# A hybrid attention layer on one core: its first projection block in another order, and the conditioning weights in smaller pieces

## The chip, the cores and the metric

The kernel runs on one core of one Trainium2 chip. Its time is the device time of one execution in microseconds; where several executions are given, the median counts. The profile is a hardware trace of one execution.

## The reference

One decoder layer on a sequence of 1,024 tokens with 1,024 channels, in float32. Cut to what matters here:

```python
mod = silu(c) @ w_ada + b_ada                      # 1024 x 6144: six vectors of 1024
shift_m, scale_m, gate_m, shift_f, scale_f, gate_f = split(mod, 6)
h    = rms(x) * (1 + scale_m) + shift_m            # adaLN: a row norm, then a scale and shift per channel
proj = h @ w_in                                    # 1024 x 4104: fq fk fv og (512 each), 8 forget logits, rq rk rv rg (512 each)
fox  = forgetting_attention(rms(fq) * g, rms(fk) * g, fv, log_sigmoid(logits + b))   # 8 heads of 64
fox  = rms(fox) * gain * sigmoid(og)
ret  = retention(rope(rq), rope(rk), rv)           # 4 heads of 128, chunks of 128
ret  = rms(ret) * gain * silu(rg)
x    = x + gate_m * (concat(fox, ret) @ w_out)
h    = rms(x) * (1 + scale_f) + shift_f
x    = x + gate_f * (square(relu(h @ w_mlp_in)) @ w_mlp_out)
```

## The kernel before, in words

Tokens are worked on in eight tiles of 128 (t = 0 to 7). Channels are split in eight slices of 128 (k = 0 to 7). A large product is done in three passes, to keep float32 accuracy: each operand is split into a rounded part and a rest (`split_w` for weights: ScalarE casts, VectorE or GpSimd subtracts, lines 133 to 135), and TensorE multiplies high by high, high by low and low by high (lines 295 to 297). A projection group (`proj_group`, line 279) takes four token tiles and 512 columns: for each k it splits one weight slice of 128x512 and runs 4 x 3 matmuls into four PSUM banks. The weights arrive two slices at a time, by SyncE's queue, into two buffers (`raw`); the split slices have five buffers (`f4`).

The input to the projections is `hT[k]`, the normalised and modulated input, turned so that channels lie on the partitions, in a rounded part and a rest. Tile t of x gets its row norm (`norm_x`: squares on ScalarE, the factor by a power on GpSimd, the product on VectorE). `make_hT(k, half)` then turns four tiles of slice k by TensorE, scales and shifts them on ScalarE with the two adaLN columns of k (`mod(0, k)`, `mod(1, k)`), casts on VectorE and subtracts on GpSimd.

The first block is the group rg. Its first half (tiles 0 to 3) needs the adaLN columns of shift_m and scale_m, slice by slice: `first_stage(k)` loads further weights, multiplies the eight rows of `ada_m[k]` (1 MB) by silu(c) and adds them up on VectorE (`ada_sum`, lines 207 to 211, and line 562), sums over the partitions by one-column matmuls (line 217), adds the bias (line 219) and calls `make_hT(k, 0)`. `ahead` runs this one slice ahead of the matmuls. The second half (tiles 4 to 7) only needs `make_hT(k, 1)`. Each half ends with `evac_rg` for its tiles: a sigmoid on ScalarE, a product on VectorE, a product with the gain on GpSimd (lines 384 to 386).

The other four adaLN vectors (16 MB of weights) are not needed until much later. `ada_stages` (line 221) makes eight pieces of 512 columns, each in two loads of 1 MB by SyncE's queue into two buffers (`mr`), with their sums on VectorE (lines 233 to 235), one-column matmuls (line 243) and a bias (line 245). Hooks at each k of the groups rq, rk and rv call these steps one after the other (`todo`, line 523).

The order of instructions on each queue is set by a planner that lists them by program order and by when it expects them to be ready; so steps of the adaLN pieces come earlier than the program writes them. Only the attention part is written as a fixed order (`manual_schedule`, line 860). After the first block come the forget logits (line 410), the groups rq, rk and rv (with rope on GpSimd and VectorE, lines 370 to 373), then the other groups, attention, the output projection and the MLP.

Of the kernel before, what the change touches and what calls it, by code (L numbers as in the profile page):

```python
# [11 lines left out]
F32 = mybir.dt.float32  # L12
# [37 lines left out]
def tile_block(  # L50
# [89 lines left out]
    pT = ctx.enter_context(tc.tile_pool(name="pT", bufs=2, space=PSUM))  # L140
# [9 lines left out]

    def tbank(name):
        return pT.tile([P, CH], F32, tag="T", name=name)
# [23 lines left out]
    early, xg = [], [None] * 4  # L176
# [8 lines left out]
    def load_first_w():  # L185
        wr = raw([P, 2, CH], "wr_first")
        Q.dma_start(wr, win_v[:, 0:2, OFF_R + 3 * RW : OFF_R + 4 * RW])
        early.append(wr)

    load_ada_m(0)  # L190
    load_x(0)
    load_x(1)
    load_first_w()
    load_ada_m(1)
    load_ada_m(2)
    load_ada_m(3)
# [8 lines left out]
    def ada_sum(w):  # L205

        for j in range(2):
            V.tensor_scalar(w[:, j], w[:, j], c_act[:, j : j + 1], None, op0=ALU.mult)
        for j in range(2, 8):
            a = w[:, j % 2]  # L210
            V.scalar_tensor_tensor(a, w[:, j], c_act[:, j : j + 1], a, op0=ALU.mult, op1=ALU.add)

    def ada_cols(w, ms, k, n):
        ps = xbank(f"mps{ms[0]}_{k}")
        for i, m in enumerate(ms):
            for j in range(n):
                T.matmul(ps[:, i : i + 1], w[:, j, i, :], ones, start=(j == 0), stop=(j == n - 1))
        for i, m in enumerate(ms):
            V.tensor_tensor(mod(m, k), ps[:, i : i + 1], bT[:, 8 * m + k : 8 * m + k + 1], op=ALU.add)

    def ada_stages(m, kq):


        ws = []

        def load(a):
            w = mr([P, 4, CH], f"wa{m}_{kq}{a}")
            Q.dma_start(w, wada_v[:, 4 * a : 4 * a + 4, m * D + kq * CH : m * D + (kq + 1) * CH])
            ws.append(w)

        def sums(a):
            w = ws[a]
            V.tensor_scalar(w[:, 0], w[:, 0], c_act[:, 4 * a : 4 * a + 1], None, op0=ALU.mult)
            for j in range(1, 4):
                V.scalar_tensor_tensor(
                    w[:, 0], w[:, j], c_act[:, 4 * a + j : 4 * a + j + 1], w[:, 0], op0=ALU.mult, op1=ALU.add
                )

        def cols_():
            ps = xbank(f"mps{m}_{kq}")  # L240
            for i in range(4):
                for a in range(2):
                    T.matmul(ps[:, i : i + 1], ws[a][:, 0, i * P : (i + 1) * P], ones, start=(a == 0), stop=(a == 1))
            at = slice(8 * m + 4 * kq, 8 * m + 4 * kq + 4)
            V.tensor_tensor(mcol[:, at], ps[:, 0:4], bT[:, at], op=ALU.add)

        return load, sums, cols_

    def norm_x(t):
        xt = xg[t // 2][:, t % 2, :]  # L250
        rr = r_x[:, t : t + 1]
        A.activation(ra([P, D], f"xsq{t}"), xt, AF.Square, accum_out=rr)
        V.tensor_scalar(rr, rr, 1.0 / D, EPS, op0=ALU.mult, op1=ALU.add)
        rsqrt_(rr, 1)
        V.tensor_scalar(xt, xt, rr, None, op0=ALU.mult)

    hT = {}

    def make_hT(k, half):

        if k not in hT:
            hT[k] = s8([P, 2, S], f"hT{k}", F32R)
        ht = hT[k]
        tp = rbank(f"tp{k}_{half}")
        for i in range(4):
            t = 4 * half + i
            T.transpose(tp[:, i * P : (i + 1) * P], xg[t // 2][:, t % 2, k * P : (k + 1) * P], ident)
        h32 = t2([P, CH], f"h32_{k}_{half}")
        A.activation(h32, tp, AF.Identity, bias=mod(0, k), scale=mod(1, k))
        hs = slice(half * CH, (half + 1) * CH)  # L270
        V.tensor_copy(ht[:, 0, hs], h32)
        G.tensor_tensor(ht[:, 1, hs], h32, f32(ht[:, 0, hs]), op=ALU.subtract)
# [6 lines left out]
    def proj_group(name, col, half, evac, hook=None, banks=None):  # L279
# [3 lines left out]
        for k in range(NK):  # L283
            if hook:
                hook(k)
            if k % 2 == 0:
                wr = early.pop(0) if early else load_win(k, col, f"{name}{half}")
            ws = f4([P, 2, CH], f"ws_{name}{half}_{k}", F32R)
            split_w(wr[:, k % 2, :], ws[:, 0, :], ws[:, 1, :], G if name == "rg" and half == 0 else V)
# [233 lines left out]
    todo = [[] for _ in range(5 * 8 + 4)]  # L523
    for n in range(8):
        load, sums, cols_ = ada_stages(2 + n // 2, n % 2)
        todo[5 * n] += [lambda load=load: load(0)]
        todo[5 * n + 2] += [lambda load=load: load(1), lambda sums=sums: sums(0)]
        todo[5 * n + 4] += [lambda sums=sums: sums(1)]
        todo[5 * n + 6 if n < 7 else -1] += [cols_]
# [15 lines left out]
    def ahead(stage):  # L545
        def go(k):
            if k == 0:
                stage(0)
            if k + 1 < NK:
                stage(k + 1)  # L550

        return go

    def first_stage(k):
        if k == 2:
            load_x(2)
        if k == 3:
            load_x(3)
        if k + 4 < NK:
            load_ada_m(k + 4)  # L560
# [5 lines left out]
    for t in range(4):  # L566
        norm_x(t)
# [551 lines left out]
```

## Time and profile before

| | us |
|---|---|
| median of three runs | 1442.01 (1440.3 to 1445.68) |
| the profiled execution | 1444.74 |
| its span in the trace | 1442.9 |

| engine | busy us | share of the span |
|---|---|---|
| TensorE (PE) | 1376.8 | 95% |
| TensorE weight loads (PEld) | 1122.7 | 78% |
| VectorE (DVE) | 636.2 | 44% |
| ScalarE (ACT) | 425.1 | 29% |
| GpSimd (POOL) | 463.9 | 32% |

Busy times are unions of the instructions' intervals; PE's matmuls overlap each other, so the start of one to the start of the next tells the pace. The clock that is granted to TensorE has two levels; a mean between them says how much of a stretch was at which. SP is SyncE, whose queue issues the DMAs. A time in brackets at the end of a line is the idle time of the engine just before it, with what ended it.

### The profile page before, as it was taken

The numbers are of one execution on the slowest core, as the hardware profiler recorded it, in microseconds if no ns is written. First come the engines' busy times: TensorE is split into PE (matmuls) and PEld (weight loads), VectorE is DVE, ScalarE is ACT, GpSimd is POOL, SyncE is SP. The second block draws the span as 40 slices with busy tenths as digits, with TensorE's granted clock in tenths as the row PEclk, the third lists the DMA queues.
The fourth block names the chain that finished last, engine by engine and source line by source line (L and its number), as shares of the span: only waits on it lengthen the run. The fifth ranks groups of instructions, "written<-read, shape, count | busy, mean of one in ns | idle before, by whom it ended". The sixth has DMA issues, their size and how long they took to land.

```text
span 1442.9 us, 17046 instructions
## 1 busy us (share of the span) xinstructions
PE 1376.8 (95%) x6581; PEld 1122.7 (78%) x6581; DVE 636.2 (44%) x1123; ACT 425.1 (29%) x757; POOL 463.9 (32%) x428
## 2 busy tenths in 40 slices
PE   4699898999999889999999999999999999999998
PEld 3477777888888667678778888888888888888887
DVE  6974777445443457753682222322223222122221
ACT  2332212233333357652343311133112321123210
POOL 3456733136452012322562421124301242013420
PEclk9889998999999989999999999999999999999999
DMA  9747446543346644942231111111112111111121
GB/s 286 218 125 168 137 115 186 126 98 117 85 128 148 166 117 118 285 176 74 89 102 30 59 46 56 44 45 59 44 44 58 45 44 57 47 44 51 52 103 59
DMA packets 109953, 146.09 MB, mean 101 GB/s; under 512 B 7624, under 2 KB 61976, under 8 KB 108848
## 3 DMA queue, kind: packets, MB, share of 16 engines
q1 hardware_dynamic: 109872, 145.00, 35.3%
q8 instruction: 52, 0.85, 0.2%
q14 instruction: 29, 0.24, 0.0%
HBM read 122.85 MB, written 10.60 MB: 92 GB/s over the span
## 4 chain that ended last, share of the span: by engine, by line
PE 54%; DVE 2%; POOL 1%; issue 0%; ACT 0%; DMA 0%; DVEq 0%; POOLq 0%; ACTq 0%
PE up L1035 8%; PE up L1036 8%; PE up L1037 8%; PE po_dn L936 8%; PE po_dn L934 8%; PE po_dn L935 8%; PE po_woA L935 1%; PE po_woA L934 1%; PE po_woA L936 1%; DVE xr L980 1%; PE av L734 1%; POOL x L944 0%; PE pt L725 0%; DVE x L940 0%; PE h2p L987 0%
## 5 line engine op out<-in xcount | busy, mean ns | idle before, releaser
L936 PE MATMUL po_dn<-ws_dn,u 128*128 128x512 f32 x512 | 199.3, 389 | 0.0
L935 PE MATMUL po_dn<-ws_dn,u 128*128 128x512 f32 x512 | 199.2, 389 | 0.0
L934 PE MATMUL po_dn<-ws_dn,u 128*128 128x512 f32 x512 | 198.0, 389 | 0.0
L1035 PE MATMUL up<-h,wuh 128*128 128x512 f32 x496 | 193.7, 391 | 0.0
L1036 PE MATMUL up<-h,wuh 128*128 128x512 f32 x496 | 193.4, 390 | 0.0
L1037 PE MATMUL up<-h,wul 128*128 128x512 f32 x496 | 193.2, 390 | 0.0
L1043 POOL TENSOR_TENSOR u<-rl,u 128x512 fp32r<-128x512 f32 x64 | 82.3, 1287 | 325.2 <-ACT u L1042 325.2
L135 DVE TENSOR_TENSOR ws_dn<-wr_dn,ws_dn 128x512 fp32r<-128x512 f32 x64 | 55.2, 862 | 204.8 <-ACT ws_dn L134 204.8
L927 POOL TENSOR_TENSOR wr_dn<-wr_dn,gf 128x512 f32<-128x512 f32 x64 | 85.9, 1364 | 155.1 <-DMA wr_dn<-in_w_mlp_out_dram 155.1
L935 PEld LDWEIGHTS po_dn<-ws_dn,u 128*128 128x128 f32 x512 | 96.1, 188 | 20.0
L936 PEld LDWEIGHTS po_dn<-ws_dn,u 128*128 128x128 f32 x512 | 96.1, 188 | 19.9
L934 PEld LDWEIGHTS po_dn<-ws_dn,u 128*128 128x128 f32 x512 | 96.1, 188 | 19.9
L134 ACT CAST ws_dn<-wr_dn 128x512 fp32r<-128x512 f32 x64 | 39.7, 620 | 242.8 <-PE po_dn L936 216.4
L1036 PEld LDWEIGHTS up<-h,wuh 128*128 128x128 f32 x496 | 93.4, 188 | 19.4
L1035 PEld LDWEIGHTS up<-h,wuh 128*128 128x128 f32 x496 | 93.4, 189 | 19.2
L1037 PEld LDWEIGHTS up<-h,wul 128*128 128x128 f32 x496 | 93.2, 188 | 19.3
L131 POOL TENSOR_TENSOR sm<-sm 128x8 f32<-128x8 f32 (+2 forms) x48 | 59.3, 1241 | 146.8 <-DVE sm L500 56.6
L135 DVE TENSOR_TENSOR wul<-wu,wuh 128x1024 fp32r<-128x1024 f32 x31 | 39.8, 1284 | 139.8 <-ACT wuh L134 111.1
L1041 DVE SCALAR_TENSOR_TENSOR rl<-up,rl 128x512 f32<-128x512 f32 x64 | 43.9, 687 | 110.7 <-ACT rl L1040 110.7
L134 ACT CAST wuh<-wu 128x1024 fp32r<-128x1024 f32 x31 | 32.7, 1054 | 123.2 <-PE up L1036 73.1
L1040 ACT ACTIVATE rl<-up 128x512 f32<-128x512 f32 x64 | 38.0, 594 | 95.6 <-PE up L1037 95.6
L940 DVE TENSOR_TENSOR x<-po_dn,x 128x512 f32<-128x512 f32 x64 | 41.6, 684 | 54.5 <-PE po_dn L936 54.5
(273 smaller groups left out, 2727.0 us busy)
## 6 DMA issues: line engine op xcount, KB each, us to landing
wa<-in_w_ada_dram SPq DMA_DIRECT2D x16, 1024.0 KB, 10.0
wu<-in_w_mlp_in_dram SPq DMA_DIRECT2D x32, 512.0 KB, 4.2
wr_dn<-in_w_mlp_out_dram SPq DMA_DIRECT2D x32, 512.0 KB, 3.5
wam<-in_w_ada_dram SPq DMA_DIRECT2D x16, 512.0 KB
x<-in_x_dram SPq DMA_DIRECT2D x8, 512.0 KB, 7.7
wr_rq<-in_w_in_dram SPq DMA_DIRECT2D x8, 512.0 KB, 6.1
wr_rk<-in_w_in_dram SPq DMA_DIRECT2D x8, 512.0 KB, 4.1
wr_rv<-in_w_in_dram SPq DMA_DIRECT2D x8, 512.0 KB, 5.0
```

The lines of the kernel that those rows point to most:

```text
L131: G.tensor_tensor(ap, ap, mhalf.to_broadcast([P, n]), op=ALU.pow)
L134: A.copy(h_ap, raw_ap)
L135: eng.tensor_tensor(l_ap, raw_ap, f32(h_ap), op=ALU.subtract)
L927: G.tensor_tensor(w, w, gate[:, cs_], op=ALU.mult)
L934: T.matmul(ps[t], lh, ws[:, 0, :], start=(kk == 0), stop=False)
L935: T.matmul(ps[t], lh, ws[:, 1, :], start=False, stop=False)
L936: T.matmul(ps[t], ll, ws[:, 0, :], start=False, stop=(kk == nk - 1))
L1035: T.matmul(ps, wh[:, k, :], hh, start=(k == 0), stop=False)
L1036: T.matmul(ps, wh[:, k, :], hl, start=False, stop=False)
L1037: T.matmul(ps, wl[:, k, :], hh, start=False, stop=(k == NK - 1))
L1041: V.scalar_tensor_tensor(rl, ps, 0.0, rl, op0=ALU.max, op1=ALU.mult)
L1043: G.tensor_tensor(u[:, 1, hs], rl, f32(u[:, 0, hs]), op=ALU.subtract)
```

## The change

The first block takes six token tiles (`FIRST`) through all eight slices and then the other two (`REST`), and is written as a fixed order on all five queues, SyncE's too. The products of the adaLN rows 0 and 1 by silu(c) go from VectorE to ScalarE (`ada_mul`); the two partial sums are added by the one-column matmuls, which are twice as many per slice. Tiles 4 and 5 of a slice are turned, scaled and split after tiles 0 to 3. VectorE does the six accumulations of slice n + 1 two by two between the casts of slice n. GpSimd subtracts for the weights in the first pass, VectorE in the second. The group's weights are loaded twice, as before.

The other adaLN vectors come in 16 pieces of 256 columns, each one load of 1 MB (eight rows), issued by ScalarE, behind what is written before it on that queue; loads, sums and column matmuls are called by the same hooks, at steps 2.5 apart. Some small loads of constants are held behind what is written before them on SyncE's queue. The two banks of the PSUM pool pT are taken strictly in turn (`Ta`, `Tb`).

```diff
+    turn_t = ["Tb", "Ta"]
     def tbank(name):
-        return pT.tile([P, CH], F32, tag="T", name=name)
+        turn_t.append(turn_t.pop(0))
+        return pT.tile([P, CH], F32, tag=turn_t[0], name=name)
...
     def ada_stages(m, kq):
+        w = mr([P, 8, 2 * P], f"wa{m}_{kq}")
+        def load():
+            at = m * D + kq * 2 * P
+            tc.keep_in_program_order(A.dma_start(w, wada_v[:, :, at : at + 2 * P]))
+        def sums():
+            V.tensor_scalar(w[:, 0], w[:, 0], c_act[:, 0:1], None, op0=ALU.mult)
+            for j in range(1, 8):
+                V.scalar_tensor_tensor(w[:, 0], w[:, j], c_act[:, j : j + 1], w[:, 0], op0=ALU.mult, op1=ALU.add)
         def cols_():
             ps = xbank(f"mps{m}_{kq}")
+            for i in range(2):
+                T.matmul(ps[:, i : i + 1], w[:, 0, i * P : (i + 1) * P], ones, start=True, stop=True)
...
+    for n in range(16):
+        todo[5 * n // 2].append(begin)                                        # load
+        todo[5 * n // 2 + 3].append(lambda stages=stages: stages[1]())        # sums
+        todo[5 * n // 2 + 5].insert(0, lambda stages=stages: stages[2]())     # columns
...
+    FIRST, REST = range(6), range(6, 8)
+    def ada_mul(k):
+        w = ada_m[k]
+        for j in range(2):
+            A.mul(w[:, j], w[:, j], c_act[:, j : j + 1])
+    def ada_acc(k, js):
+        w = ada_m[k]
+        for j in js:
+            V.scalar_tensor_tensor(w[:, j % 2], w[:, j], c_act[:, j : j + 1], w[:, j % 2], op0=ALU.mult, op1=ALU.add)
+    def ada_mps(k):
+        mp_of[k] = xbank(f"mps{k}")
+        for m in range(2):
+            for j in range(2):
+                T.matmul(mp_of[k][:, m : m + 1], ada_m[k][:, j, m, :], ones, start=(j == 0), stop=(j == 1))
...
+    with tc.manual_schedule(engines={ENG.PE, ENG.Activation, ENG.DVE, ENG.Pool, ENG.SP}):
...
+        times("rg0", 0, range(4))
+        turn_x(0, (4, 5), xbank)
+        scaled(0, (4, 5))
+        split_h(0, (4, 5))
+        for k in range(NK):
+            n = k + 1
+            if n < NK:
...
+                turn_x(n, range(4), tag_bank("Ta"))
+                ada_mps(n)
+                ada_add(n)
+                scaled(n, range(4))
+                split_first_w("rg0", n, G)
+                if n + 1 < NK:
+                    ada_mul(n + 1)
+                    ada_acc(n + 1, range(2, 4))
+                split_h(n, range(4))
             if k == 0:
+                times("rg0", 0, (4, 5))
+            else:
+                times("rg0", k, (0, 1))
+            if n < NK:
+                turn_x(n, (4, 5), xbank)
+                scaled(n, (4, 5))
+                if n + 1 < NK:
+                    ada_acc(n + 1, range(4, 6))
+                split_h(n, (4, 5))
+                if n + 1 < NK:
+                    ada_acc(n + 1, range(6, 8))
+            if k:
+                times("rg0", k, range(2, 6))
...
+            if k == 7:
+                load_first_w("rg1", 2)
+                for m in range(2):
+                    turn_x(m, REST, (tag_bank("Ta"), xbank)[m])
+                    scaled(m, REST)
+                    split_h(m, REST)
+                    split_first_w("rg1", m, V)
+        tabs["ret"] = load_gain(ret_gain)
+        for t in FIRST:
+            evac_rg(t, ps_of[t])
+        for t in REST:
+            ps_of[t] = bank(f"pp_rg_{t}")
+        for k in range(NK):
+            if k + 2 < NK:
+                if k in (2, 4):
+                    load_first_w("rg1", k + 2)
+                turn_x(k + 2, REST, (tag_bank("Ta"), xbank)[k % 2])
+                scaled(k + 2, REST)
+                split_h(k + 2, REST)
+                split_first_w("rg1", k + 2, V)
+            times("rg1", k, REST)
+        for t in REST:
+            evac_rg(t, ps_of[t])
+    tc.keep_in_program_order(Q.dma_start(rc, rconst))
```

The helpers `square`, `factor`, `norm`, `turn_x`, `scaled`, `split_h`, `split_first_w` and `times` hold the instructions of `norm_x`, `make_hT`, `split_w` and the three matmuls, one step each.

## Rows read from the trace of the kernel before

**Rows 1.** Windows by stage: PE, PEld, DVE, ACT, POOL busy, clock, DMA.

```profile
20.30:79.90 59.60, 43.13 (x178) 33.26 (x177) 53.26 (x109) 18.00 (x29) 25.65 (x21) 0.86 0.84 247
...
84.30:108.70 24.40, 24.36 (x105) 20.14 (x105) 17.94 (x23) 6.32 (x10) 11.72 (x9) 0.93 0.41 84
...
116.70:271.00 154.30, 143.03 (x658) 118.44 (x658) 109.23 (x154) 32.53 (x55) 70.90 (x56) 0.94 0.54 147
```

**Rows 2.** Timeline of DVE and POOL, first block: start, us, engine, line.

```profile
21.40 2.45 DVE L211 SCALAR_TENSOR_TENSOR wam<-wam,sm 128x256 f32<-128x256 f32 x6
...
64.44 4.50 DVE L211 SCALAR_TENSOR_TENSOR wam<-wam,sm 128x256 f32<-128x256 f32 x6
...
64.33 2.74 POOL L135 TENSOR_TENSOR ws_rg<-wr_rg,ws_rg 128x512 fp32r<-128x512 f32 x2
```

**Rows 3.** Windows and timeline where DVE is full and TensorE waits.

```profile
150.00:161.00 11.00, 6.99 (x24) 5.31 (x23) 10.89 (x15) 0.77 (x2) 9.25 (x13) 0.84 0.15 38
...
227.00:238.00 11.00, 11.00 (x40) 9.30 (x40) 10.96 (x12) 0.99 (x2) 10.43 (x8) 0.65 0.78 259
...
219.84 0.48 DVE L233 TENSOR_SCALAR wa<-wa,sm 128x512 f32<-128x512 f32 x1 [7.88 <-DMA wa<-in_w_ada_dram]
...
223.26 0.35 PE L243 MATMUL mps<-sm,wa 128*128 128x1 f32 x2 [2.84 <-issue]
...
226.45 3.15 PE L243 MATMUL mps<-sm,wa 128*128 128x1 f32 x14 [2.34 <-DVE wa L235]
```

**Rows 4.** Windows of line 243 alone: PE and PEld busy, clock, DMA.

```profile
109.60:272.00 162.40, 13.02 (x96) 13.58 (x96) 0.95 0.56 153
```

**Rows 5.** Timeline and groups: prices of single steps (groups: busy, mean ns).

```profile
61.38 0.22 DVE L219 TENSOR_TENSOR sm<-mps,sm 128x1 f32<-128x1 f32 x2 [0.44 <-PE mps L217]
...
61.72 0.78 ACT L269 ACTIVATE h<-tp,sm 128x512 f32<-128x512 f32 x1 [4.57 <-DVE sm L219]
62.40 2.17 ACT L134 CAST ws_rg<-wr_rg 128x512 fp32r<-128x512 f32 x4
...
62.53 0.43 DVE L271 CAST hT<-h 128x512 fp32r<-128x512 f32 x1 [0.17 <-ACT h L269]
...
L337 ACT COPY fv<-pp_fv 128x256 f32<-128x256 f32 x8 | 2.8, 370 | 1.3 <-PE pp_fv L297 1.2
...
L272 POOL TENSOR_TENSOR hT<-h,hT 128x512 fp32r<-128x512 f32 x16 | 23.1, 1450 | 29.9 <-DVE hT L271 29.9
...
L135 POOL TENSOR_TENSOR ws_rg<-wr_rg,ws_rg 128x512 fp32r<-128x512 f32 x6 | 8.2, 1387 | 0.0
```

**Rows 6.** Timeline of PE: neighbouring matmuls at the low and the high clock.

```profile
30.07 0.63 PE L296 MATMUL pp_rg<-ws_rg,hT 128*128 128x512 f32 x1
30.49 0.63 PE L295 MATMUL pp_rg<-ws_rg,hT 128*128 128x512 f32 x1
...
37.35 0.40 PE L297 MATMUL pp_rg<-ws_rg,hT 128*128 128x512 f32 x1
37.58 0.39 PE L296 MATMUL pp_rg<-ws_rg,hT 128*128 128x512 f32 x1
```

**Rows 7.** Timeline: POOL's gain products; PE at the end of the fixed order.

```profile
84.78 6.09 POOL L386 TENSOR_TENSOR gr<-gr,ain_in_ret_out_gain_dram 128x512 f32<-128x512 f32 x4
...
640.33 0.50 PE L934 MATMUL po_woA<-ws_woA,mixr 128*128 128x512 f32 x1
...
644.18 0.87 PE L734 MATMUL av<-pT,fv 128*64 128x256 f32 x8
```

**Rows 8.** Windows of lines 235, 233 and 211 alone: DVE busy, clock, DMA.

```profile
116.70:271.00 154.30, 30.36 (x36) 0.94 0.54 147
...
116.70:271.00 154.30, 8.32 (x12) 0.94 0.54 147
...
20.30:79.90 59.60, 22.58 (x42) 0.86 0.84 247
```

**Rows 9.** Timeline of SP's queue: the issue of two 512 KB loads.

```profile
1.70 1.37 SPq L174 DMA_DIRECT2D wam<-in_w_ada_dram  x2
```

More of the change, by code (lines that the diff above doesn't have):

```diff
@@ L203, in tile_block @@
         V.tensor_scalar(bT[:, 8 * m : 8 * m + 8], bT[:, 8 * m : 8 * m + 8], 1.0, None, op0=ALU.add)
[L205 to L219, printed above, removed]
@@ L239, in cols_ @@
         def cols_():
             ps = xbank(f"mps{m}_{kq}")
[L241 to L245, printed above, removed]
-        return load, sums, cols_
[L249 to L255, printed above, removed]
@@ L520, in tile_block, with begin @@
     ret = retention()
[L523 to L529, printed above, removed]
+    todo = [[] for _ in range(44)]
+    for n in range(16):
+        stages = []
+        def begin(n=n, stages=stages):
+            stages += ada_stages(2 + n // 4, n % 4)
+            stages[0]()
+        todo[5 * n // 2].append(begin)
+        todo[5 * n // 2 + 3].append(lambda stages=stages: stages[1]())
+        todo[5 * n // 2 + 5].insert(0, lambda stages=stages: stages[2]())
     todo = [[]] + todo
@@ L542, in ret_hook @@
         return go
-    def ahead(stage):
-        def go(k):
-            if k == 0:
[L548 to L560, printed above, removed]
-        ada_sum(ada_m[k])
-        V.tensor_tensor(ada_m[k][:, 0], ada_m[k][:, 0], ada_m[k][:, 1], op=ALU.add)
-        ada_cols(ada_m[k], [0, 1], k, 1)
-        make_hT(k, 0)
@@ L566, in tile_block @@
[L566 to L573 removed]
+    FIRST, REST = range(6), range(6, 8)
+    W6 = len(FIRST) * P
+    ws_of, ps_of, h32_of, tp_of, mp_of = {}, {}, {}, {}, {}
+    def ada_mul(k):
+        w = ada_m[k]
+        for j in range(2):
+            A.mul(w[:, j], w[:, j], c_act[:, j : j + 1])
@@ new lines, in square, with factor, norm, turn_x @@
+    def square(t):
+        A.activation(ra([P, D], f"xsq{t}"), xg[t // 2][:, t % 2, :], AF.Square, accum_out=r_x[:, t : t + 1])
+    def factor(t):
+        rr = r_x[:, t : t + 1]
+        V.tensor_scalar(rr, rr, 1.0 / D, EPS, op0=ALU.mult, op1=ALU.add)
+        rsqrt_(rr, 1)
+    def norm(t):
+        xt = xg[t // 2][:, t % 2, :]
+        V.tensor_scalar(xt, xt, r_x[:, t : t + 1], None, op0=ALU.mult)
+    def turn_x(k, toks, bank_):
+        if k not in hT:
+            hT[k] = s8([P, 2, S], f"hT{k}", F32R)
+        tp = tp_of[k, toks[0]] = bank_(f"tp{k}_{toks[0]}")
+        for i, t in enumerate(toks):
+            T.transpose(tp[:, i * P : (i + 1) * P], xg[t // 2][:, t % 2, k * P : (k + 1) * P], ident)
@@ new lines, in times, with tag_bank @@
+    def times(name, k, toks):
+        ws = ws_of[name, k]
+        for t in toks:
+            hh = hT[k][:, 0, t * P : (t + 1) * P]
+            hl = hT[k][:, 1, t * P : (t + 1) * P]
+            T.matmul(ps_of[t], hh, ws[:, 0, :], start=(k == 0), stop=False)
+            T.matmul(ps_of[t], hh, ws[:, 1, :], start=False, stop=False)
+            T.matmul(ps_of[t], hl, ws[:, 0, :], start=False, stop=(k == NK - 1))
+    def tag_bank(tag):
+        return lambda name: pT.tile([P, CH], F32, tag=tag, name=name)
```

127 lines of the change are left out of this document (78 added, 49 removed).

## The prediction

> **What bounds the kernel now.** I read the page's busy shares first: TensorE (PE) is busy 95% of the span, so only stretches where it idles or runs at its lower clock can give time. The windows by stage come next [rows 1]. From 20.3 to 79.9 us, the first half of rg with its adaLN columns (four token tiles, eight rounds, one per k), PE is busy 43.1 of 59.6 us at a granted clock of 0.86, while VectorE (DVE) is busy 53.3. 4.4 us later, from 84.3 to 108.7, the second half runs almost without a gap, 24.4 us. The forget logits take the 8.0 to 116.7. From there to 271 (rq, rk, rv) PE idles 11.3 us and its clock is 0.94, so 154.3 x 0.06 = 9.3 us more are lost. After that PE hardly waits until attention. So the change can win in two places: the first block (before 108.7) and the rq-to-rv stretch.
>
> Why the first block is slow: six accumulations of 128x256 take 2.45 us alone, but 4.50 us beside two GpSimd (POOL) subtractions of 2.74 us together [rows 2]. 2.05 of the 2.74 us went from DVE, three quarters. Before, DVE's work of a round (two products, six accumulations, an add, a cast) and this loss fill the round of about 7.5 us; DVE is the bound.
>
> Where PE waits later: between 150 and 161 it is busy 6.99 of 11 us while DVE is busy 10.89; four stretches of 11 us (from 150, 172, 194 and 227) have DVE at 9.8 to 11.0, the first and the last stand [rows 3]. At 219.84 DVE had sat 7.88 us behind a 1 MB adaLN piece that had not landed, with weight subtractions queued behind it; PE idled 2.84 us and the clock of the last stretch is 0.65.
>
> **The change, part by part.** The first block becomes one fixed order on five queues: six token tiles with the adaLN columns, then two.
>
> A round, from the ada column products of k to those of k+1. DVE's share is now six accumulations and two casts (four and two tiles): 2.45 + 0.4 + 0.25 = 3.1 us alone (a cast of four tiles 0.43 [rows 5], of two an estimate), the products having gone to ScalarE (ACT). But these accumulations wait for a chain in the new order: 8 one-column matmuls (0.14 us each, 13.02/96 [rows 4], 1.1 us), the add 0.22, scaling 0.7 (ACT starts the next instruction 0.68 later), the weight cast 0.6, the product by c 0.37 [rows 5]. That is 3.0 us plus 0.1 of hand-overs, 3.1 us in which DVE has only the add. A 256-wide product from SBUF on ACT is not in this trace: 0.37 (copy from PSUM) is the nearest row, 0.62 (the cast of twice the width) the upper end; I take 0.37.
> POOL has three subtractions in a round: weights 1.39, four tiles 1.45, two tiles half of that, 0.7, in all 3.5 us [rows 5]. Three quarters of that on DVE are 2.6, less 0.5 for what falls before the first accumulation and after the last. Round: 3.1 + 3.1 + 2.1 = 8.3 us. From below it is PE's own work: 18 matmuls at 0.23 [rows 6], 1.1, six transposes at about 0.12 = 5.9, or 6.2 for chain plus DVE with no loss; from above, with all of POOL's time lost, 3.1 + 3.1 + 3.5 - 0.4 = 9.3. I take 8.3, because the loss is measured on the very same instructions.
> The Trainium skill, "SBUF — State Buffer", Terms, has DVE and GpSimd take one port pair by an exclusive lock for a whole instruction, so that the loser fully blocks; by that the round is the 9.3 us and the sum 6.0 us higher. The trace agrees in kind, with 75% of POOL's time lost, not all.
>
> The head is the old one to 20.3; with 12 matmuls at the low clock (0.43 each, 5.2 us [rows 6]) and the transposes of tiles 4 and 5 the first round begins at 26.8, an estimate. Six rounds lead to 26.8 + 49.8 = 76.6; then 1.1, 36 matmuls (8.2) and 0.25: six tiles are done at T = 86.1. The old order has four at 79.9.
> The clock: in a round PE idles 2.4 us, once. Two matmul starts are 0.42 us apart around 30 us and 0.23 at 37 [rows 6]; at the low level a round's PE work is 11.8 us, 3.5 more than the round. None to six such rounds: 0 to +21 us; I take +2, less than one, since in the old block PE's gaps were a larger share and its clock was still 0.86.
>
> The last two tiles. The evacuation of six tiles stands in the order ahead of the rounds k = 2 to 7 of tiles 6 and 7. From T: transposes and two scalings with two casts on ACT 3.2 us, a sigmoid and DVE's product 1.2 (estimates from the ACT rows of [rows 5]): POOL starts its six gain products at T + 4.4. Four of them took 6.09 us [rows 7], 1.52 each, so 9.1 us: until T + 13.5. Only then comes POOL's subtraction for k = 2 (0.7), which the third of its matmuls needs: T + 14.3. PE has done k = 0 and 1 by about T + 8 and stands. What is left is 34 matmuls (7.8 us), transposes 1.5, and about 2.6 at the low clock: the end is T + 26.2 = 112.3, against 108.7: **+3.6 us**. With POOL out of the way it would be T + 13.9, with the products slower T + 28.
> PE's gap there need not stay empty: outside work did slip between fixed-order instructions before. Output-projection matmuls start at 640.33 while the fixed order's last av group is at 644.18 [rows 7]. The forget logits of tiles 0 to 3 are ready, half of 8.0 us: **-4.0** (0 if the planner sees no gap).
>
> The adaLN pieces, 256 columns and 16 loads of 1 MB instead of 8 pieces in two halves, now all behind the block. One-column matmuls: the code makes 128 before, of which 96 lay after 109.6 [rows 4]; 64 now, all after: 32 x 0.136 = **-4.3**. DVE: before, 36 accumulations (30.4 us) and 12 products (8.3) lay in rq to rv [rows 8]. Now there are 112 and 16 of half the width: at 0.41 and about 0.3 alone 50.7 us, at the first block's mean of 0.54 (22.58/42 [rows 8]) and 0.4, 66.9. So +12 to +28 us of DVE; I take 20. Where DVE is saturated, 44 of 154 us, it reaches PE: 20 x 0.29 = **+6** (0 if the 45 us in which DVE idles take it, +28 if none of it hides).
> Loads on ACT's queue: an issue of 1,024 packets took SP 0.69 us (two in 1.37 [rows 9]), 16 are 11 us on an ACT that is busy 32.5 of 154. An issue waits until the piece two before it is used up, and behind it stand weight casts, for which DVE and then PE wait. Cover: casts run up to three steps ahead. If that is gone, 14 issues x (0.62 + 0.69) = 18 us; I take 0. Gain: weight loads on SP no longer stand behind adaLN pieces, and a piece is one load, not two together. What the late piece at 219.84 cost PE is 2.84 + 2.34 in two waits and 11 x 0.35 = 3.9 of clock [rows 3]: 9 us; I take half, **-4.5**, between 0 and -9.
> The Trainium skill, "DMA: Bandwidth & Descriptors", Issuing engines are not separate DMA queues, says that transfers of all issuers share the same 16 engines and a second issuer saves only issue time; by that the -4.5 is 0. No run here shows a load from ACT.
>
> At nothing: rconst, gains and bias loads behind SP's rg loads (six issues, hidden since rk's evacuation and the logits come later; without cover 4.1 us at the 0.69 of [rows 9]); the PSUM tags Ta and Tb in turn (two banks as before); the square and factor of tiles 6 and 7 (ACT and DVE idle in a round; without that some 3 us, an estimate).
>
> Sum: +3.6 + 2 - 4.0 - 4.3 + 6 - 4.5 = -1.2 us. The profiled execution took 1444.7 (span 1442.9); the three runs' median is 1442.0, so 1443.5 by the one, **1441** by the other. A measurement of this kernel can tell about 0.5% (7.2 us) from no change.
>
> **Rivals.**
> 1. *The rounds run at PE's pace.* The fixed order puts POOL's subtractions where DVE waits for the chain, a round is 6.2 us (six rounds -12.6), no round is at the low clock (-2), and the late-piece stalls go altogether (-4.5): -20, **1422**. For it: the old order left POOL and DVE to collide by chance, and DVE sheds work. Against: two of three subtractions follow a DVE cast and meet the next accumulations.
> 2. *DVE becomes the bound in rq and rk (slower).* The place is where the rope's POOL products block DVE, 150 to 238 us. All 28 us arrive at PE (+22 more than taken), the loads bring no relief (+4.5), a lead of three weight steps (36 matmuls, 8.3 us) is spent once: +17, **1459**. It decides as soon as adaLN's DVE work of a group of 22 us, about 11, with weights 5.5, rope 5 to 6 and POOL's blocking, passes 22. For: [rows 3]. Against: 45 us of idle DVE, mostly in rq's start and rv.
> 3. *The pipeline doesn't do what it says:* POOL's products block DVE for their whole time (9.3 a round, +6.0) and the last gap stays empty (+4.0): +8.8, **1451**.
>
> **Chances.** My forecast, no change, 0.36 (own range 1433 to 1448); rival 1 0.32, rival 2 0.20, rival 3 0.12. Range 1419 to 1459. Faster by over 0.5% (under 1434.8): 0.30 of rival 1 and 0.06 of the forecast, 0.36. Slower (over 1449.2): 0.19 + 0.08 + 0.02 = 0.29. Within: 0.35.
>
> **What would show it.** In the new profile: starts of one k's ada columns 8.3 us apart (6.2: rival 1; 9.3: rival 3); the last matmul of six tiles near 86; six POOL gain products in a row and PE waiting for a POOL subtraction at k = 2 of tiles 6 and 7; forget-logit matmuls inside that gap; rq's first matmul at 114 to 118; DVE over 9 of 11 us through rq1 to rk1 with PE waiting for weight subtractions (rival 2); no DVE wait of several us for an adaLN piece. Wrong if rq starts before 108, or if PE idles over 20 us between rq's start and rv's end.

## The result, and the profile after

The kernel after is slower: 1458.2 us (median, 1454.5 to 1463.1) against 1441.2 for the kernel before on the same chip, 1.0107 of it by the ratio on record (95% interval 1.0084 to 1.0130; the two medians of four executions each would give 1.0118). Timed a second time it stood at 1.0099 (1.0080 to 1.0118). The forecast was 1441, no change. The profiled executions are 11.3 us apart (1456.0 against 1444.7; spans 1454.1 and 1442.9), so they show two thirds of the loss.

Where it lies is read from the starts of matmuls (us from the start of the span):

| start of | before | after | later by |
|---|---|---|---|
| last matmul of rg | 108.3 | 110.8 | +2.5 |
| first forget logit | 109.3 | 115.0 | +5.7 |
| first of rq | 116.8 | 124.0 | +7.2 |
| first of fq | 289.9 | 299.5 | +9.6 |
| first of the output projection | 640.3 | 653.0 | +12.7 |
| end of the span | 1442.9 | 1454.1 | +11.2 |

So 7.2 us are lost ahead of rq and 5.5 us more between rq and the output projection; behind that the kernel after is 1.5 us shorter. The windows of the kernel after, six tiles, then two, then rq's first matmul to fq's (span, then busy time of PE, PEld, DVE, ACT, POOL, granted clock, DMA share, GB/s):

```profile
26.05:86.70 60.65, 49.03 (x228) 39.98 (x229) 36.28 (x70) 19.32 (x37) 27.38 (x24) 0.89 0.51 137
86.70:111.20 24.50, 17.93 (x65) 13.21 (x62) 17.50 (x24) 11.95 (x24) 15.53 (x14) 0.79 0.38 86
123.90:299.50 175.60, 157.11 (x723) 127.72 (x721) 134.40 (x245) 37.85 (x64) 76.71 (x57) 0.96 0.59 160
```

Against [rows 1]: VectorE, full in the old block, has 24 us to spare in the new rounds; and the last two tiles leave PE idle 6.6 us at a clock of 0.79, where the old second half had no gap. From rq to fq VectorE now has 134.4 us of work. The same stretch of the kernel before:

```profile
116.80:289.90 173.10, 161.03 (x754) 134.12 (x753) 115.41 (x164) 38.24 (x64) 73.01 (x57) 0.94 0.53 140
```

PE has 4 us less to do now, and idles 18.5 in place of 12.1; VectorE has 19.0 us more.

A round of the six tiles, from the timeline (start, us, engine, line):

```profile
51.48 0.35 PE L523 MATMUL mps<-sm,wam 128*128 128x1 f32 x2 [1.63 <-issue]
...
53.17 0.23 DVE L527 TENSOR_TENSOR sm<-mps,sm 128x1 f32<-128x1 f32 x2 [0.92 <-PE mps L523]
...
54.88 1.28 POOL L135 TENSOR_TENSOR ws_rg<-wr_rg,ws_rg 128x512 fp32r<-128x512 f32 x1 [2.90 <-ACT ws_rg L134]
55.24 1.59 DVE L517 SCALAR_TENSOR_TENSOR wam<-wam,sm 128x256 f32<-128x256 f32 x2 [1.84 <-ACT wam L512]
...
57.09 1.90 DVE L517 SCALAR_TENSOR_TENSOR wam<-wam,sm 128x256 f32<-128x256 f32 x2
57.25 1.46 POOL L557 TENSOR_TENSOR hT<-h,hT 128x512 fp32r<-128x512 f32 x1 [1.09 <-DVE hT L556]
...
59.12 1.34 DVE L517 SCALAR_TENSOR_TENSOR wam<-wam,sm 128x256 f32<-128x256 f32 x2
59.27 0.90 POOL L557 TENSOR_TENSOR hT<-h,hT 128x256 fp32r<-128x256 f32 x1 [0.56 <-DVE hT L556]
59.69 0.35 PE L523 MATMUL mps<-sm,wam 128*128 128x1 f32 x2
```

Each pair of accumulations meets one of POOL's three subtractions, and the three pairs take 4.83 us where six alone took 2.45 [rows 2]. Rounds begin at 26.05, 34.47, 43.28, 51.48, 59.69, 68.24 and 76.51: 8.4 us on average.

The end of the block, and the forget logits:

```profile
90.75 8.01 POOL L340 TENSOR_TENSOR gr<-gr,ain_in_ret_out_gain_dram 128x512 f32<-128x512 f32 x6
...
99.94 0.79 PE L570 MATMUL pp_rg<-ws_rg,hT 128*128 128x512 f32 x1 [3.03 <-POOL hT L557]
...
107.79 0.33 DVE L352 MEMSET wfr<- 128x320 f32 x1
108.14 2.08 SPq L354 DMA_DIRECT2D wfr<-in_w_in_dram  x2
...
113.90 0.33 DVE L356 CAST wf<-wfr 128x320 fp32r<-128x320 f32 x1 [1.39 <-DMA wfr<-in_w_in_dram]
...
115.02 0.43 PE L364 MATMUL fp<-hT,wf 128*40 128x512 f32 x1 [3.81 <-DVE wf L357]
```

PE stands for POOL's six products, as forecast. But the logits, which were to fill that gap, begin only at 115.02: their weights are cleared and loaded at 108, behind all of SyncE's fixed order and nearly all of VectorE's, and PE stands a second time, 3.81 us. In the kernel before the same load was issued at 96.70, and the weights were cast 6 us ahead of rg's last matmul (108.3):

```profile
96.70 0.99 SPq L400 DMA_DIRECT2D wfr<-in_w_in_dram  x2
...
102.13 0.33 DVE L402 CAST wf<-wfr 128x320 fp32r<-128x320 f32 x1 [3.71 <-DMA wfr<-in_w_in_dram]
```

In rk, VectorE beside POOL's rope products, from the timeline:

```profile
211.11 1.47 POOL L324 TENSOR_TENSOR ac_rk<-rk,cs 128x512 f32<-128x512 f32 x1 [1.76 <-DVE sm L222]
...
211.35 1.52 DVE L326 TENSOR_TENSOR rk<-ac_rk,as_rk 128x256 f32<-128x256 f32 x1
...
212.53 1.48 POOL L325 TENSOR_TENSOR as_rk<-rk,cs 128x512 f32<-128x512 f32 x1
...
212.79 1.51 DVE L327 TENSOR_TENSOR rk<-as_rk,ac_rk 128x256 f32<-128x256 f32 x1
...
214.22 3.84 DVE L215 SCALAR_TENSOR_TENSOR wa<-wa,sm 128x256 f32<-128x256 f32 x4
...
214.44 1.40 POOL L324 TENSOR_TENSOR ac_rk<-rk,cs 128x512 f32<-128x512 f32 x1 [0.42 <-DVE rk L327]
...
215.80 1.46 POOL L325 TENSOR_TENSOR as_rk<-rk,cs 128x512 f32<-128x512 f32 x1
...
217.98 0.42 DVE L326 TENSOR_TENSOR rk<-ac_rk,as_rk 128x256 f32<-128x256 f32 x1
...
218.91 0.48 DVE L215 SCALAR_TENSOR_TENSOR wa<-wa,sm 128x256 f32<-128x256 f32 x1
...
219.49 0.58 PE L220 MATMUL mps<-sm,wa 128*128 128x1 f32 x4 [2.71 <-issue]
```

The rope's sum takes 1.52 us beside POOL and 0.42 without; four adaLN additions take 3.84 where one alone takes 0.48. The weights' rest (L135) that is queued behind them comes at 219.31.

The longest waits of PE from rq to fq, after (engine, line, waited for: us, times, longest):

```profile
PE mps L220 <- issue: 6.0, 3, 2.7
PE pp_rv L249 <- DVE rk L312: 2.9, 1, 2.9
PE pp_rq L250 <- DVE ws_rq L135: 2.2, 1, 2.2
PE pp_rv L250 <- DVE ws_rv L135: 2.1, 1, 2.1
PE pp_rv L249 <- DVE rv L263: 1.8, 1, 1.8
```

For the first, the column matmuls of a piece, the profile names nothing. But each of the three ends 0.10 us behind an addition of a piece: the one at 219.49 behind the seventh, which ran from 218.91 to 219.39 (the others at 189.05 and 265.62). So by the order in time these too wait for VectorE, and so do all others.

### The profile page after: what moved, and what is told of

The parts are those of the page before. It is cut to its first block, busy times and chain, and to the rows that moved or that the text cites. A ratio compares the mean times of both kernels' runs of the same rounds, so it can differ in the third digit from the quotient of the medians.

```text
span 1454.1 us, 17086 instructions
## 1 busy us (share of the span) xinstructions
PE 1376.3 (95%) x6549; PEld 1116.5 (77%) x6549; DVE 643.5 (44%) x1179; ACT 433.5 (30%) x781; POOL 472.9 (33%) x436
## 3 DMA queue, kind: packets, MB, share of 16 engines
q1 hardware_dynamic: 101424, 128.23, 31.4%
## 4 chain that ended last, share of the span: by engine, by line
PE 54%; DVE 2%; POOL 1%; issue 0%; ACT 0%; DMA 0%; POOLq 0%; DVEq 0%; ACTq 0%
PE up L1142 8%; PE up L1143 8%; PE up L1144 8%; PE po_dn L1042 8%; PE po_dn L1043 8%; PE po_dn L1041 8%; PE po_woA L1042 1%; PE po_woA L1041 1%; PE po_woA L1043 1%; DVE xr L1087 1%; PE av L841 0%; POOL x L1051 0%; PE pt L832 0%; DVE x L1047 0%; PE po_woB L1042 0%
## 5 line engine op out<-in xcount | busy, mean ns | idle before, releaser
L135 DVE TENSOR_TENSOR ws_dn<-wr_dn,ws_dn 128x512 fp32r<-128x512 f32 x64 | 53.3, 833 | 207.5 <-ACT ws_dn L134 207.5
L135 DVE TENSOR_TENSOR wul<-wu,wuh 128x1024 fp32r<-128x1024 f32 x31 | 39.8, 1283 | 138.5 <-ACT wuh L134 109.8
L215 DVE SCALAR_TENSOR_TENSOR wa<-wa,sm 128x256 f32<-128x256 f32 x112 | 65.5, 587 | 1.7
```

Source lines behind the costliest of these rows:

```text
L135: eng.tensor_tensor(l_ap, raw_ap, f32(h_ap), op=ALU.subtract)
L215: V.scalar_tensor_tensor(w[:, 0], w[:, j], c_act[:, j : j + 1], w[:, 0], op0=ALU.mult, op1=ALU.add)
```

## The experiments

Ratios are to the kernel before, timed on the same chip; 0.001 is 1.44 us. Places are read from one profiled execution of each run, ratios from all its executions. Theory A: the block is lost in its end (late logit weights, POOL's products); theory B, later E and 2: VectorE from rq to rv. The rivals stand in the expectations.

### One half of the change at a time

```diff
 e1 = before, e2 = after with - and + exchanged:
-w = mr([P, 4, CH], ...)      Q.dma_start(w, wada_v[:, 4 * a : 4 * a + 4, ...])   # two per piece, 8 pieces
+w = mr([P, 8, 2 * P], ...)   A.dma_start(w, wada_v[:, :, at : at + 2 * P])       # one per piece, 16 pieces
```

> The kernel before with only adaLN's later pieces changed: 16 pieces of 256 columns, issued by ScalarE; the first block stays eight tiles. Theory A (the first block and the late logit weights carry most of the loss: start of rq was 7.2 us later, and the pieces cost the rest, 4 us): about 1445, between 1442 and 1449. Rival B (the pieces carry it: VectorE's extra work in rk, where the stage went from 52.2 to 60.2 us): 1450 to 1458, with the stages from rq to rv longer by 8 or more in sum. Rival C (the pieces are a gain, as the waits for the rows of wa fell): 1435 to 1440.

> The kernel after, with adaLN's pieces as they were (8 pieces of 512 columns, issued by SyncE). Theory A: the first block alone starts rq late by about 7 us, and the rest is as before: 1448 to 1454. Rival B (pieces are the cause): within 3 us of the kernel before, 1438 to 1444. If the two edits add up, this run's loss and that of the pieces alone sum to 17 us.

Measured: pieces alone 1.0033 (1.0019 to 1.0047), block alone 1.0083 (1.0058 to 1.0108). They add up to 1.0116, near the loss of both (1.0107 and 1.0099). Theory A's ranges held by the ratios: +4.8 and +12.0 us on 1441 are 1446 and 1453 (the medians were 1449.8 and 1456.9, beside 1445.2 for the kernel before). In e1's profile rq starts at 111.5, 5.3 us early: 12 additions of pieces that the old order did in the block, from 39.4 us on, are gone from it, and the first now stands at 106.3; fq starts at 291.9, 2.0 late. In e2 rq starts at 125.8, and rq to fq takes 175.5. e2's block is not quite that of after: six of the old pieces' additions slip into its second round, which then takes 10.4 us.

### The two waits at the end of the block

```diff
 e3:  if k == 6: wfr = r2(...); V.memset(wfr, 0.0); Q.dma_start(wfr, ...)   # in the six-tile rounds
      k == 7:    wf cast and subtracted on VectorE                          # not in forget_logits
 e4: -evac_rg(t, ps)        # sigmoid, product, gain product of the six tiles
     +evac_rg without POOL's gain product; six gain_rg(t) behind the rounds of tiles 6 and 7
```

> The kernel after, with the 16 columns of forget-gate weights loaded and cast in the last rounds of the first block, ahead of the loads of the last two tiles, in place of behind them. Theory A (the wait of 3.81 us at the first logits matmul is on the path): logits start right behind the last rg matmul, rq starts 3.5 to 5 us earlier (119 to 120.5), and the whole is 3 to 5 us shorter than after: 1453 to 1455. Rival D (the time is given back later, because the next stages are set by VectorE and the pieces): rq starts earlier and the whole is within 1.5 us of after.

> The kernel after, with POOL's six products by the ret gain of tiles 0 to 5 issued behind POOL's part of the last two tiles' rounds. Theory A (these 8 us of POOL stand ahead of the subtraction that the third round needs, and TensorE waits 3.03 us there): that wait goes, the last rg matmul starts 2.5 to 4 us earlier (107 to 108), but the logits' weights then bind at the same 115, unless they move with the loads; the whole 0 to 3 us shorter than after. If POOL was hidden, nothing moves.

e3 also takes the weights' buffers from another pool. Measured: e3 1.0075 (1.0049 to 1.0101), e4 1.0066 (1.0041 to 1.0091), against 1.0099 for after: 3.5 and 4.8 us better by the ratios, with intervals that overlap that of after, so the gain of either alone is not shown by its time. The places are plain in the profiles. e3's logits, from PE's timeline, do slip into the gap of the block:

```profile
99.00 0.40 PE L357 MATMUL fp<-hT,wf 128*40 128x512 f32 x1
```

and rq starts at 115.6, 8.4 us earlier than after and earlier than its forecast; fq, at 296.6, only 2.9. e4's third round waits no more (rg's last matmul at 104.5), and from 90.93 on the logits' weights are all that PE waits for, in PE's timeline:

```profile
90.93 0.65 PE L573 MATMUL pp_rg<-ws_rg,hT 128*128 128x512 f32 x1 [2.64 <-DVE gr L339]
...
111.79 0.65 PE L369 MATMUL fp<-hT,wf 128*40 128x512 f32 x1 [6.87 <-DVE wf L362]
```

In both profiles rq to fq then takes 181.0 us, 175.5 after: e3 gives back 5.5 of its 8.4 us, e4 more than the 3.3 by which its rq (120.7) is early. (The profiled execution of e3 is the fastest of its six, 1448.3.) That became the open question.

### The same edit in the kernel before

`e11`: before, with the logit weights loaded and cast ahead of the second half of rg.

> The kernel before, with the 16 columns of forget-gate weights loaded ahead of the last four tiles' norms, so that TensorE can do the logits in its gaps of the first block. If gaps can be filled (in the block of six and two the logits began at 99.0 once their weights were there): rq starts 4 to 7 us earlier, the whole 1436 to 1442. If it is given back: within 2 us of before.

1.0012 (1.0002 to 1.0022): no gain. The logits begin at 110.7 (109.3 before); PE is busy 10.0 of every 10 us from 90 to 150, so there is no gap to fill.

### What a round consists of

```diff
 e6:  -G.tensor_tensor(rest, x, high, op=subtract)   +A.copy(rest, x)     # tiles 0-5, first-pass weights
 e13: -G.tensor_tensor(rest, x, high, op=subtract)   +V.tensor_tensor(...) # hT and first-pass weights
```

> The kernel after, with the low parts of hT for tiles 0 to 5 and of the first-pass weights written by a ScalarE copy in place of POOL's subtraction (the low parts then hold the plain copies): POOL does nothing in the rounds of the first six tiles. Theory L (VectorE's accumulations of 128x256 are held up by POOL on a port that both share: 1.34 to 1.90 us a pair with POOL beside, against 2.45 for six alone): the pairs fall to 0.8 to 1.0 us and the round from 8.3 to 6.0 to 7.0 us. Rival M (the chain of ScalarE and TensorE sets the round): pairs fall, the round stays 7.5 to 8.5.

> The kernel after, with one change: the low parts of hT and of the first-pass weights in the rounds are subtracted by VectorE in place of POOL (nothing is left out). Theory L (POOL beside VectorE costs more than the subtractions are worth: the round without POOL was 5.98 us): VectorE per round has six accumulations of 0.41, two casts, three subtractions of 0.35 to 0.70 and one column sum, 5.1 to 5.5 us, and the round falls from 8.3 to 6.0 to 6.6 us; six tiles done 11 to 14 us earlier; as the logit weights still come late, the start of rq 8 to 12 us earlier, and the whole 1444 to 1451. Rival N (VectorE becomes the bound of the round): round 7.5 or more, whole within 4 us of after.

e6 leaves POOL's subtractions out and writes plain copies in their place. From the fourth on, its rounds begin at 48.21, 54.18, 60.16 and 66.14, 5.98 us apart (a single execution, 1445.8). VectorE's timeline of a round:

```profile
49.42 0.22 DVE L533 TENSOR_TENSOR sm<-mps,sm 128x1 f32<-128x1 f32 x2 [0.92 <-PE mps L529]
51.47 0.88 DVE L523 SCALAR_TENSOR_TENSOR wam<-wam,sm 128x256 f32<-128x256 f32 x2 [1.82 <-ACT wam L518]
...
52.61 0.88 DVE L523 SCALAR_TENSOR_TENSOR wam<-wam,sm 128x256 f32<-128x256 f32 x2
...
53.60 0.88 DVE L523 SCALAR_TENSOR_TENSOR wam<-wam,sm 128x256 f32<-128x256 f32 x2
```

A pair takes 0.88 without POOL: 4.83 less 2.64 is 2.2 us a round lost to POOL's 3.64 us of subtractions, 60% of them. The prediction had 2.1. Theory L holds for the rounds. e13, where nothing is left out, has rounds of 7.4 us, not 6.0 to 6.6: VectorE's pairs take 0.88 here too, but its three subtractions (0.69, 0.69, 0.43) are now in the same chain. Still 1.0040 (1.0026 to 1.0055), 8.5 us better than after, with rq at 119.3: VectorE's own 1.8 us cost less than POOL beside it, and the last two tiles no longer wait for POOL's products either, since their subtractions moved too.

### The repaired block

```diff
 e8 = e3 and e4 and, with the old pieces (e7: with the new; e12: e8 and e13's edit):
+ada_mul(n + 1)                      # ScalarE's products of the next slice, ahead of
 turn_x(n, range(4), tag_bank("Ta")) # the turned tiles' scaling
 ...
-ada_mul(n + 1)
```

> The first block of the kernel after with three repairs (logit weights early, POOL's gain products behind the last two tiles' rounds, the product by the modulation column issued on ScalarE ahead of the turned tiles' copies), and adaLN's pieces as before. Theory A (the block's loss lies in the late logit weights, the gain products and a round of 8.3 us): start of rq falls from 125.8 (block alone) to 108 to 116, and the whole to 1439 to 1447. Rival G (the block's loss is given back behind it, whenever rq starts): rq starts by 116 and the whole stays above 1450.

> The repaired block (logit weights early, gain products late, column product ahead of the copies) with adaLN's pieces as in the kernel after: 16 of 256 columns, issued by ScalarE. If edits add: the repaired block with old pieces stood at 1.0018 of the kernel before, the pieces alone at +0.0033: 1.003 to 1.006, 1448 to 1452. Rival: with the block repaired the pieces' order from ScalarE is a gain (no transfers of pieces beside the first block's): below 1443.

> The block with its three repairs, adaLN's pieces as before, and the low parts on VectorE. If the gains add: rounds of 6.0 to 6.3 us in place of 6.9, start of rq 106 to 110 (112.6 without), the whole 1438 to 1443, no slower than the kernel before. If what is gained ahead of rq is given back between rq and fq (as the pieces alone gave back 5 of 5): 1444 to 1448.

e8 1.0018 (1.0004 to 1.0032), e7 1.0002 (0.9989 to 1.0014), e12 1.0050 (1.0031 to 1.0070). The block's loss is repaired (theory A), with later rounds of 6.9 us and rq at 112.6 and 106.4. e7 came out below its forecast of 1.003 to 1.006: the new pieces, which cost 0.0033 beside the old block, cost nothing beside the repaired one. e7's rq is 10.4 us ahead of the kernel before's, its fq 2.6, and its time is the same: what is won ahead of rq goes again. e12 was a miss, outside both its ranges: e13's edit doesn't add to the others, later rounds were 7.2 to 7.5 and rq started at 117.5.

### What takes the time back: additions, bursts, place

```diff
 e10: -for j in range(1, 8):  +for j in range(1, 2):     # sums() of a late piece
 e9:  -sums() in one step      +sums of four rows in one step, four in the next
 e15, e16: e8, e7 +ada_hook(k) in each round of tiles 6 and 7   # e16: those loads not held in program order
```

> The kernel after, with one of the seven accumulations of each of adaLN's 16 later pieces kept and six left out (the modulation columns 2 to 5 then miss their terms): VectorE loses 96 additions of 0.587 us, 56 us of work, nearly all of it between the start of rq and that of fq. Theory E (VectorE's additions stand ahead of the weights' low parts that TensorE waits for, in bursts of 4.6 us): the stretch from rq to fq falls from 175.5 to 180 us to 163 to 170, and the whole by 6 to 12 us: 1446 to 1452. Rival F (the stretch is set by TensorE's clock and the transfers of wa): the stretch within 3 us, the whole within 3 us of after, 1455 to 1461.

> The kernel after, with each piece's eight steps on VectorE given out in two bursts of four, one round of the projection apart, the work unchanged. Theory E1 (the burst of 4.6 us, longer than the 3.2 us of before, is what delays the weights' low parts): the waits of pp_rq, pp_rk and pp_rv on VectorE's subtractions fall by half, 3 to 6 us off the whole: 1452 to 1455. Rival E2 (the sum of the work counts, not its bursts): within 2 us of after.

> The repaired block with adaLN's old pieces (8 of 512 columns), and the first eight steps of their schedule taken in the last two tiles' rounds, ahead of rq. Theory 1 (pieces that the kernel before did inside its first block are what lengthens rq to rv): the stretch from rq to fq falls from 179.7 to 171 to 175 us, rq starts at 112 to 115, and the whole is 1439 to 1443. Rival (their additions delay the last two tiles' rounds by as much): rq starts 3 us or more later, the whole within 2 us of the repaired block's 1.0018.

> The same with the new pieces (256 columns, ScalarE): theory 1: the whole 3 to 6 us below the repaired block with new pieces. Rival: within 2 us of it.

e10, which leaves out six of a piece's seven additions: 1.0035 (1.0018 to 1.0052), 9 us better than after, as theory E had it for the whole; but in the profile, of the slowest of its ten executions, rq to fq takes 172.8 us, 2.7 to 5.4 less than in the two profiles of after and not the 163 to 170 of its forecast. The additions' sum matters; where, this run doesn't show. e9: 1.0078 (1.0054 to 1.0101), 3 us better than after with intervals that overlap: E1's 3 to 6 us and E2's no change are not told apart, and PE's waits for VectorE's subtractions did not fall by half (5.6 us, 4.7 after). e15 1.0030 (1.0018 to 1.0042) and e16 1.0038 (1.0025 to 1.0051) are no better than e8 and e7 without the hooks (e16 is worse by 5 us), and rq to fq took 182.2 and 191.1 us, longer and not shorter: the place of the pieces, theory 1, falls.

### POOL's rope products

```diff
-G.tensor_tensor(ac, dv, cos, op=ALU.mult)      +V.tensor_tensor(ac, dv, cos, op=ALU.mult)
-G.tensor_tensor(as_, dv, sin, op=ALU.mult)     +V.tensor_tensor(as_, dv, sin, op=ALU.mult)
```

`e17` on after, `e18` on e7, `e19` on before.

> The kernel after, with the 32 rotary products of rq and rk (128x512) on VectorE in place of POOL. Theory 2 (VectorE is held up while POOL runs its products): the mean of the 128x256 additions falls from 0.587 to below 0.50 us, VectorE's busy time between rq and fq grows by less than the 21 us that 32 products of 0.67 us add (to 135 to 147), and the whole is the same or up to 6 us shorter than after. Rival: VectorE, with 21 us more, delays the weights' low parts: 3 to 10 us longer than after.

> The kernel before, with the 32 rotary products on VectorE. If the price stood in the kernel before as well: the stretch from rq to fq falls from 173.1 to 150 to 158 us, the whole to 1422 to 1430. Rival (it is the change's own, from 112 additions in place of 36): the stretch falls by less than 6 us, the whole 1437 to 1443.

> The repaired block with new pieces, and the 32 rotary products on VectorE. If both add: 1.0002 less 0.0166 (0.9933 against 1.0099), 0.983 to 0.986 of the kernel before, 1418 to 1423 us, with rq at 105 to 108 and fq at 256 to 260. Rival (what is won ahead of rq is given back): 1428 to 1434.

e17: **0.9933** (0.9913 to 0.9953), 1432.4 us, 24 us below after. Its first block is that of after (rq at 123.8). The window from there to fq:

```profile
123.80:274.10 150.30, 145.72 (x689) 119.81 (x688) 119.17 (x252) 37.17 (x63) 23.34 (x25) 1.00 0.69 177
```

25 us shorter, PE idle 4.6 us in place of 18.5, clock 1.00 in place of 0.96 (33 matmuls fewer lie in it; but up to the output projection the gain is 25.2 us too). VectorE got 32 products of 0.69 us more, 22 us, and is busy 119.2 us in place of 134.4; 14 additions, 6.8 us, moved out of the window. The group of adaLN additions, after and then e17 (busy, mean ns, idle before):

```profile
L215 DVE SCALAR_TENSOR_TENSOR wa<-wa,sm 128x256 f32<-128x256 f32 x105 | 62.1, 594 | 1.6
```

```profile
L215 DVE SCALAR_TENSOR_TENSOR wa<-wa,sm 128x256 f32<-128x256 f32 x91 | 41.9, 483 | 1.0
```

Theory 2 holds, with a gain four times its upper end, and with VectorE's busy time not at 135 to 147 but below that of after. e19: 0.9915 (0.9901 to 0.9930): the price stood in the kernel before too, though smaller (0.0085, 12 us) and less than its forecast. Its window:

```profile
116.20:276.20 160.00, 156.71 (x753) 131.37 (x752) 112.17 (x197) 37.98 (x65) 26.05 (x25) 0.97 0.60 152
```

e18: **0.9855** (0.9829 to 0.9881), 1422.5 us against 1443.0: both gains add within the intervals, and this version beats both kernels by 20 us and more. Against e19, the same edit on the kernel before, it is 9 us shorter (1422.5 and 1431.6 on one chip, with intervals that do not meet): repaired, and with POOL out of the way, the change is a gain. Its fq, at 263.1, missed the 256 to 260 of the forecast: rq to fq takes 156.4 us, 150.3 in e17, so some of what is won ahead of rq still goes.

How much VectorE loses beside the rope's products is read from groups with the same work in two runs. Two groups of the kernel before, each followed by the same in e19:

```profile
L235 DVE SCALAR_TENSOR_TENSOR wa<-wa,sm 128x512 f32<-128x512 f32 x36 | 30.4, 852 | 0.4
```

```profile
L235 DVE SCALAR_TENSOR_TENSOR wa<-wa,sm 128x512 f32<-128x512 f32 x36 | 26.6, 745 | 0.2
```

```profile
L372 DVE TENSOR_TENSOR rk<-ac_rk,as_rk 128x256 f32<-128x256 f32 x8 | 7.6, 948 | 0.0
```

```profile
L372 DVE TENSOR_TENSOR rk<-ac_rk,as_rk 128x256 f32<-128x256 f32 x8 | 3.3, 418 | 0.0
```

Over all groups, the instructions of VectorE from rq to fq are longer beside the products by some 21 us in after (against e17; 12 of them on the additions) and some 24 in before (against e19; 14 of them on the rope's own sums). So the loss is about the same in both kernels. But from rq to the output projection e17 is 25.2 us shorter than after, e19 only 13.7 shorter than before: with the added work, more of the same loss reaches PE. VectorE idles 41 us of the stretch from rq to fq in after and 58 in before, which fits; no run varies that by itself. The runs also move POOL's longer way through the rope (1.47 a product against 0.69 on VectorE), and do not separate it. The rows speak for VectorE's lengthening: its waits for a rope product are 3.6 us in after and 7.6 in before, and PE waits for none.

### After, once more

> The kernel after, unchanged, timed beside the others: 1.008 to 1.012 of the kernel before, as the first time (1.0107). A second profile of it shows how far the stage lengths differ from one execution to another: start of rq at 123 to 126, the stretch from rq to fq 174 to 181 us.

1.0099. Its profiled execution lies at the upper end of its spread (span 1460.4). One thing that differs is the clock in the rounds. Window from 50 to 80 us, after and then e0:

```profile
50.00:80.00 30.00, 24.47 (x114) 19.79 (x115) 20.10 (x40) 11.02 (x22) 13.48 (x14) 0.89 0.25 66
```

```profile
50.00:80.00 30.00, 25.41 (x108) 20.84 (x107) 19.99 (x39) 9.93 (x19) 13.52 (x13) 0.77 0.26 69
```

e0's rounds are 8.7 us apart on average, 8.4 in the other, and rg's last matmul is 2.0 us later; 1.9 us more come in the wait for the logits (6.1 us from rg's last matmul, 4.2 in the other) and 1.1 in the logits. So rq starts at 129.0 in e0, beyond its forecast, and at 124.0 in the other: a profile's place of rq is known to 5 us only, and the comparisons above rest on the ratios where they can.

## Why the prediction was wrong, point by point

**Right:**
- *Round 8.3 us, six tiles done at 86.1:* 8.4 and about 86.7. The three parts (chain 3.1, VectorE 3.1, lost to POOL 2.1) are those of the profile, and e6 shows the last at 2.2. The rounds of rivals 1 and 3 (6.2 and 9.3) are out; 6.2 is indeed near what a round costs once POOL is out (5.98). The other half of rival 3, the empty gap, is what happened.
- *Last two tiles +3.6:* +2.5, by the mechanism given: six products of POOL (8.01 us, 1.34 each, not 1.52), the third round waiting. e4 takes the wait away.
- *One-column matmuls -4.3:* from rq to fq they kept PE busy 13.0 us before and 8.8 after, and PE's whole busy time fell from 161.0 to 157.0.
- *Clock +2 of 0 to +21:* of the right size as far as the profiles show: 0.89 in one, 0.77 in the other over the same 30 us, with rg's end 2.0 us apart.

**Wrong, first step: "The forget logits of tiles 0 to 3 are ready ... -4.0".** Tiles were ready; the logits' weights were not. I looked only at what PE waits for in hT, and not at the load, the clearing and the cast that the same call issues on SyncE and VectorE, which the fixed order put behind the last two tiles. In place of -4.0 there came 3.2 us of waiting (rg's end to the first logit: 4.2 us, 1.0 before) and 1.6 us of low clock in the logits (8.8 us from first to last, 7.2 before; eight starts in a row are 0.43 us apart, in place of 0.23). With the weights early (e3) the logits went into the gap. Ahead of rq the sum was to be +1.6 and was +7.2.

**Wrong, second step: "20 x 0.29 = +6" for VectorE's work from rq to rv.** The place was right, it is rival 2's ("where the rope's POOL products block DVE"), and so was the work as a whole: VectorE is busy 19.0 us longer from rq to fq. (The pieces alone rose by 31.4 us, 62.1 + 8.0 for 30.4 + 8.3, above the forecast's 28; the rope's sums fell by 9.8, 18.1 for 27.9.) Too small was the part of it that reaches PE, which was taken from the share of time in which VectorE is full. Measured by difference: from rq's first matmul to that of the output projection, after takes 529.0 us and before 523.5, +5.5; with the rope's products off POOL they take 503.8 (e17) and 509.8 (e19), -6.0. So meeting POOL costs the change 11.5 us, about twice the +6 (these are four single profiles, but the ratios say the same: 0.0166 less 0.0085, 12 us), and without it the pieces are worth -6.0, where -4.3 and -4.5 were to give -8.8. With POOL out of the way the change is neutral as a whole, within the intervals: 0.9933 against 0.9915. What the share missed: the loss to POOL, some 21 to 24 us in either kernel, reached PE by about half before and wholly after. That the added work used up the idle time in which it was hidden is argued from the rows, not shown by a run. Additions that meet POOL are held up (0.594 against 0.483 us on average), the weights' rests queue behind them, and PE's wait is followed by low clock (0.94 and 0.96 with the products on POOL, 0.97 and 1.00 without).

*Loads -4.5:* not shown. PE's waits at the pieces' column matmuls, which this term was to shorten, are 6.2 us in sum, 5.2 before. VectorE's waits for a piece's rows are shorter (longest 4.2 us, 7.9 before), but in sum 15.9 us against 17.4: the change of queue brings the pieces hardly sooner to where VectorE needs them. That is what the Trainium skill, "DMA: Bandwidth & Descriptors", Issuing engines are not separate DMA queues, had it: another issuer saves only the issue.

Rival 2's 1459 is what was measured, but by luck and not by its sum: more than half of the loss (7.2 of 12.7 us) lies ahead of rq, where it had nothing, and of its 28 us about 11.5 arrived.

## What to carry to other kernels

When a step is to slip into a gap, follow everything that its call issues (load, clearing, cast) on every queue, not only the operand that the gap is named after. Work added to VectorE is priced by what runs on GpSimd beside it: count GpSimd's time in the stretch. Here 60 to 75% of it was lost to VectorE where VectorE worked without a pause, and some 40 to 47% over all of rq to fq (21 of 53 us of rope products after, 24 of 50 before); a loss of which half stays hidden can reach TensorE whole once work is added. Try those GpSimd instructions on VectorE first; here a two-line edit gained 12 us in the kernel before and 24 in the kernel after, and the pipeline, once repaired, nothing by itself and 9 us beside that edit. Time won ahead of a stretch that another engine paces was largely given back there, so repair that stretch first.

## What was not expected of the hardware

Moving 32 products of 128x512 from GpSimd (1.40 to 1.48 us each between 211 and 217 us, 1.45 to 2.06 on the mean of a group) to VectorE (0.69) left VectorE with less busy time between rq and fq, not more, even with the 6.8 us that moved away counted in: 126.0 us for 134.4, while its additions fell from 0.594 to 0.483 us. Between 211.1 and 218.1 us of the kernel after, VectorE took 6.87 us for two rope sums and four additions that cost 2.76 alone (2 x 0.42 + 4 x 0.48): 4.1 us lost to four GpSimd products of 5.8 us, 71%, near the 75% of [rows 2] and above the 60% of a round. The Trainium skill, "SBUF — State Buffer", Terms, describes an exclusive lock held for a whole instruction; the runs agree in kind and show less than all of GpSimd's time lost. Not every instruction of VectorE pays: products that read PSUM (L312) take 0.68 us with the rope's products on GpSimd and 0.68 without, and two of them took 1.28 us from 205.57 beside a GpSimd product of 1.47 us that began at 205.33.
